# A two-layer transformer trunk: how the Down stage forms its weight sums, and when its first pieces are split

## The chip, the cores and the metric

The kernel runs on one core of a Trainium2 chip. A core has five engines with an instruction queue each: TensorE (PE, matrix products into PSUM banks), VectorE (DVE), ScalarE (ACT), GpSimd (POOL) and SyncE (SP), which issues most DMA transfers. Each queue runs in its written order. The metric is the device time of one execution in microseconds. The numbers come from that time and from the profile of one execution.

## The reference, cut to what matters

The trunk has two layers over 512 positions of width 1024. Each layer is an attention block and a SwiGLU block (FFN), each between an RMS norm before and after:

```
h = rms_norm(x, ffn_pre_g[layer])
f = (silu(h @ w_gate) * (h @ w_up)) @ w_down      # 1024 -> 2816 -> 1024
x = x + rms_norm(f, ffn_post_g[layer])
```

After layer 0, a shared key/value projection (w_kv_shared) is taken from x, for the attention of layer 1. All data are float32. For precision, each float32 operand is split into a high half and the rest, and a product is made of three matmuls: high by high, high by low, low by high.

## The kernel before, in words

**Split.** `split` (L143) makes the high half on ACT (a cast, L144) and the low half on DVE (a subtraction, L145). Weights give `whi` and `wlo`, hidden pieces `ph` and `pl`. `split_scaled` (L147) does the same with a factor per partition.

**Feed.** The class `Feed` brings the weights of the whole program in order. `load` issues the transfers some steps ahead. `split` (the method, L289) forms the sums a step needs, takes a pair of `hi`/`lo` tiles (three pairs are there) and splits. `next` asks for the split of the steps ahead of the one that PE takes now. Three weight streams matter here: `Pair` (gate and up weights of two hidden blocks), `Down` (w_down) and the plain chunks of w_v, whose gain was multiplied into the raw weights by DVE (L305) before the split.

**Pairs.** The hidden width is 22 blocks of 128. The first four are made whole, the other 18 in nine pairs (`products`, L1323) with a seven-product scheme that saves one product in eight. After each product j, ACT and DVE carry its banks into the tiles `gt` and `ut`; after j = 6 the two hidden blocks `hd` are finished (L1365 to L1369). `Hidden.add` (L1099) then forms their sums `hs` (L1113 to L1116).

**Down.** `down` (L1128) multiplies the hidden blocks by w_down with the same scheme. w_down is cut into four quarters: A11, A12, A21, A22. The seven products have the weights A11, A12, A22, E1, E2, E3, E6 in this order, with

```
E1 = A22 + A21,  E3 = A21 + A11,  E2 = E1 + A11,  E6 = E2 + A12
```

Each weight comes in six tiles (five of 1024 columns, a last one of 512), so Down has 42 steps: step 6 j + i is tile i of product j. A full step is 12 matmuls of 512 columns, a last one 6. Tiles 4 and 5 go together. The piece of step s + 2 is split when PE takes step s (`ahead`, L1135), and so is its weight.

**Where the sums came from.** A11 and A12 lie in tiles of 1024 (A12's last three in tiles of the pool "u"), and all were handed on as columns of 512. A22 is loaded to "u" tiles on SP (L218). E1 was made in place: once A22's tile was split, POOL issued a transfer that adds A21 from memory onto it (L231). For E3, SP loaded A21 to tiles with the tag "h", which hidden blocks leave, and POOL issued transfers that add A11 onto it. So a layer had 22 accumulating transfers. E2 and E6 are DVE sums (L236), tied to the steps 16 + 2 e and 27 + 2 e.

**After a product.** `After` (L1197) gathers the products into four row tiles of y: copies by ACT (L1211), sums by DVE (L1216), squares by ACT (L1221). After E3 rows 0 and 1 are whole, after E6 rows 2 and 3. `rstd` adds up the squares (L1249, L1250), takes the power -1/2 on POOL (L1252) and scales. In layer 0, `turn` (L1268) transposes the scaled y by PE (`yt`) and adds it to x; it stands in E6 behind group 2. In layer 1 (`AfterLast`), x is transposed by PE (`xt`, L1305) in E2, y gets its gain (L1311), and DVE scales, adds x (L1319) and stores the result (L1321).

**Buffers.** The pool "u" has 40 tiles of 128 x 512. Pieces, y tiles, x tiles, gate tiles and A22 share it.

**Order.** The program names engines and data. A planner with a cost model of its own puts the instructions of each engine and queue in an order, by program order among those it believes ready. So an instruction may stand earlier in a queue than the program has it, and the queue then holds whatever is behind it until its operands are there.

Of the kernel before, what the change touches and what calls it, by code (L numbers as in the profile page):

```python
# [68 lines left out]
def trunk(ctx: ExitStack, tc: tile.TileContext, a, out):  # L69
# [117 lines left out]
    class Down:  # L187
# [7 lines left out]

        def __init__(self, src):
            self.src, self.at = src, {}
# [5 lines left out]
        def quarter(self, j):  # L203
            return {self.A11: 0, self.A12: 1, self.A22: 3, self.E3: 2}.get(j)

        def load(self, j, i):
            q = self.quarter(j)
            if q is None:
                return
            n = self.width(i)  # L210
            src = self.src[q, i]
            tag = {self.A11: "raw" if i < 5 else "sum", self.A12: ("sum", "sum2", "sum2", "u", "u", "u")[i],
                   self.A22: "u", self.E3: "h"}[j]
# [6 lines left out]
            else:  # L220
# [8 lines left out]
        def accumulate(self, parts, q, i):  # L229
            for c, t in enumerate(parts):  # L230
                nc.gpsimd.dma_start(t, self.src[q, i, :, c * S:c * S + S], accum_op=OP.add)  # L231

        def plus(self, j, i, x, y):

            for t, u in zip(self.at[y, i], self.at[x, i]):
                V.tensor_tensor(t, t, u, op=OP.add)  # L236
            self.at[j, i] = self.at[y, i]

        def sums(self, j, i):

            s = self.TILES * j + i
            for e in range(self.TILES):
                if s == 16 + 2 * e:
                    self.plus(self.E2, e, self.E1, self.A11)
                if s == 27 + 2 * e:
                    self.plus(self.E6, e, self.E2, self.A12)

        def later(self, j, i):
            if j == self.A22:
                self.accumulate(self.at[j, i], 2, i)  # L250
                self.at[self.E1, i] = self.at[j, i]

    class Feed:
# [35 lines left out]
        def split(self, i):  # L289
            while len(self.ready) <= min(i, len(self.plan) - 1):  # L290
# [9 lines left out]
                elif isinstance(src, Pair):  # L300
                    src.sums(gain)
                    raw = src.raw[gain]
                elif gain is not None:
                    rv = raw[:, :n].rearrange("p (a b) -> p a b", a=gain.shape[1])
                    V.tensor_tensor(rv, rv, gain, op=OP.mult)  # L305
                if room is None:
# [4 lines left out]
                if isinstance(raw, list):  # L311
                    for c, t in enumerate(raw):
                        c_ = slice(c * S, c * S + S)
                        split(pieces[0][0][:, c_], pieces[0][1][:, c_], t)
                    src.later(*gain)
                for c in range(0, 0 if isinstance(raw, list) else n, w):
                    m = min(w, n - c)
                    with ExitStack() as st:
                        for b in self.behind.get(j, ()):
                            st.enter_context(tc.issue_after(b.ins))  # L320
                        split(pieces[c // w][0][:, :m], pieces[c // w][1][:, :m], raw[:, c:c + m])
# [392 lines left out]
    def plan_v(c):  # L714
        gv = gqk.rearrange("p (k t) -> p k t", t=2)
        for kc in range(4):
            feed.add(a["w_v"][c, kc], 1024, gv[:, 2 * kc:2 * kc + 2, 1:2].to_broadcast([P, 2, S]),
# [291 lines left out]
    def ffn(i, x_src, osp, firsts):  # L1009
# [73 lines left out]
        down(hid.pieces, post)  # L1083
# [3 lines left out]
    class Hidden:  # L1087
# [3 lines left out]
        def __init__(self, make):  # L1091
            self.make, self.n, self.t, self.two = make, 0, [], None
            self.pieces = {j: [] for j in range(7)}

# [33 lines left out]
    def down(pieces, post):  # L1128
# [3 lines left out]
        steps = [(j, i) for j in range(7) for i in range(Down.TILES)]  # L1132
        ready = {}

        def ahead(n):  # L1135
            while len(ready) <= min(n, len(steps) - 1):
                j, i = steps[len(ready)]
                h, l = U(F32R, "ph"), U(F32R, "pl")
                at = 0
                for t in pieces[j][i]:  # L1140
                    n_ = t.shape[1]
                    split(h[:, at:at + n_], l[:, at:at + n_], t)
                    at += n_
                ready[j, i] = h, l

        at = 0
        for j in range(7):
            to = (al, ga, de, be, al, al, be)[j]
            for group in ((0,), (1,), (2,), (3,), (4, 5)):
                got = []  # L1150
                for i in group:
                    ahead(at + 2 - len(got))
                    w = feed.next(Down.width(i), 2 - len(got))
                    got.append((i, w, ready[j, i]))
# [42 lines left out]
    class After:  # L1197
# [48 lines left out]
        def rstd(self, h):  # L1246
            q = slice(2 * h, 2 * h + 2)
            one, two = (1, 0) if h else (0, 1)
# [364 lines left out]
```

## Time and profile before

| what | us |
|---|---|
| median of 3 runs (1185.35 to 1186.72) | 1186.59 |
| profiled execution | 1186.21 |
| its span, first to last instruction | 1184.1 |
| PE, DVE, ACT, POOL busy | 1128.8, 947.1, 686.2, 62.5 |
| Down stage of layer 0, first matmul to the last of E6 | 425 to 554 |
| Down stage of layer 1 | 1040 to 1176 |

The span is what the trace shows; about 2 us of the time lie around it. "Idle before" a group is time in which its engine had nothing to run, with what ended it. PE's busy time holds matmuls that run at a low granted clock, so a full PE isn't always a fast one.

### The profile page before, as it was taken

The numbers are of one execution on the slowest core, as the hardware profiler recorded it, in microseconds if no ns is written. First come the engines' busy times: TensorE is split into PE (matmuls) and PEld (weight loads), VectorE is DVE, ScalarE is ACT, GpSimd is POOL, SyncE is SP. The second block draws the span as 40 slices with busy tenths as digits, with TensorE's granted clock in tenths as the row PEclk, the third lists the DMA queues.
The fourth block names the chain that finished last, engine by engine and source line by source line (L and its number), as shares of the span: only waits on it lengthen the run. The fifth ranks groups of instructions, "written<-read, shape, count | busy, mean of one in ns | idle before, by whom it ended". The sixth has DMA issues, their size and how long they took to land.

```text
span 1184.1 us, 18971 instructions
## 1 busy us (share of the span) xinstructions
PE 1128.8 (95%) x6973; PEld 998.9 (84%) x6973; DVE 947.1 (80%) x1712; ACT 686.2 (58%) x1361; POOL 62.5 (5%) x89
## 2 busy tenths in 40 slices
PE   9999999999999989798999999999999999988895
PEld 6788889899999977586888887789899999966774
DVE  7778648998989867799858877659989899776776
ACT  6476646655555556468437766556655555554563
POOL 1200000000000013100000000000000000013100
PEclk9999999999999999899999999999999999988898
DMA  7433154223232369532456656363232323378401
GB/s 227 117 107 89 37 182 153 75 90 125 90 125 90 120 189 229 139 99 89 147 142 168 166 142 170 89 214 125 72 125 90 107 94 105 133 226 182 116 1 72
DMA packets 62269, 149.79 MB, mean 127 GB/s; under 512 B 8352, under 2 KB 9888, under 8 KB 62176
## 3 DMA queue, kind: packets, MB, share of 16 engines
q1 hardware_dynamic: 55696, 137.00, 36.8%
q0 software_dynamic: 6336, 11.54, 5.7%
q8 instruction: 55, 0.90, 0.3%
q14 instruction: 38, 0.31, 0.1%
q10 hardware_dynamic: 144, 0.04, 0.0%
HBM read 125.28 MB, written 8.59 MB: 113 GB/s over the span
## 4 chain that ended last, share of the span: by engine, by line
PE 74%; issue 9%; DVE 6%; DMA 6%; ACT 3%; POOL 2%; SPq 0%; POOLq 0%; DVEq 0%; ACTq 0%
PE al L1349 18%; PE b L346 10%; PE b L347 10%; PE b L348 9%; PE be L1349 8%; DMA wd<-in_w_down 4%; PE ga L1349 4%; PE al L1162 4%; PE be L1162 2%; PE pt L498 2%; DVE wlo L145 1%; ACT whi L144 1%; POOL wd L231 1%; PE b L1474 1%; PE sc L1466 1%
## 5 line engine op out<-in xcount | busy, mean ns | idle before, releaser
L144 ACT CAST whi<-raw 128x1024 fp32r<-128x1024 f32 (+4 forms) x262 | 235.1, 907 | 247.3 <-PE al L1349 82.9
L145 DVE TENSOR_TENSOR wlo<-raw,whi 128x1024 fp32r<-128x1024 f32 (+4 forms) x262 | 271.0, 1042 | 81.9 <-ACT whi L144 80.1
L1349 PE MATMUL al<-th,whi 128*128 128x256 f32 x432 | 124.1, 287 | 0.0
L1349 PE MATMUL al<-tl,whi 128*128 128x256 f32 x432 | 122.2, 283 | 0.0
L1349 PE MATMUL al<-th,wlo 128*128 128x256 f32 x432 | 122.1, 283 | 0.0
L346 PE MATMUL b<-xh,whi 128*128 128x512 f32 (+1 forms) x304 | 116.4, 386 | 0.6 <-ACT xh L148 0.6
L347 PE MATMUL b<-xl,whi 128*128 128x512 f32 (+1 forms) x304 | 113.0, 372 | 0.0
L348 PE MATMUL b<-xh,wlo 128*128 128x512 f32 (+1 forms) x304 | 112.7, 371 | 0.0
L174 DVE TENSOR_TENSOR raw<-raw,raw 128x1024 f32<-128x1024 f32 x72 | 86.5, 1217 | 0.3 <-DMA raw<-in_w_pair 0.2
L1349 PEld LDWEIGHTS al<-th,whi 128*128 128x128 f32 x432 | 82.7, 191 | 1.8
L1349 PEld LDWEIGHTS al<-th,wlo 128*128 128x128 f32 x432 | 82.8, 192 | 0.0
L1349 PEld LDWEIGHTS al<-tl,whi 128*128 128x128 f32 x432 | 82.7, 192 | 0.0
L144 ACT CAST whi<-wd 128x512 fp32r<-128x512 f32 x86 | 50.6, 620 | 53.7 <-PE be L1162 14.9
L486 ACT ACTIVATE p<-p,mn 128x128 f32<-128x128 f32 (+1 forms) x96 | 54.0, 563 | 31.4 <-DVE mn L484 30.9
L145 DVE TENSOR_TENSOR ptl<-pt,pth 128x128 fp32r<-128x128 f32 (+1 forms) x96 | 46.2, 485 | 28.9 <-ACT pth L144 22.9
L145 DVE TENSOR_TENSOR wlo<-wd,whi 128x512 fp32r<-128x512 f32 x86 | 56.7, 685 | 14.6 <-ACT whi L144 14.6
L346 PEld LDWEIGHTS b<-xh,whi 128*128 128x128 f32 x304 | 57.6, 190 | 8.8 <-ACT xh L148 1.9
L231 POOL DMA_DIRECT2D wd<-in_w_down x44 | 39.0, 922 | 492.7 <-DMA wd<-in_w_down 222.7
L348 PEld LDWEIGHTS b<-xh,wlo 128*128 128x128 f32 x304 | 57.4, 189 | 8.9
L347 PEld LDWEIGHTS b<-xl,whi 128*128 128x128 f32 x304 | 57.7, 190 | 7.0 <-DVE xl L149 0.3
L1162 PE MATMUL al<-whi,ph 128*128 128x512 f32 x132 | 53.5, 405 | 8.6 <-ACT ph L144 7.0
L144 ACT CAST pth<-pt 128x128 fp32r<-128x128 f32 (+1 forms) x96 | 40.3, 424 | 28.7 <-PE pt L498 28.0
(301 smaller groups left out, 3297.8 us busy)
## 6 DMA issues: line engine op xcount, KB each, us to landing
raw<-in_w_pair SPq DMA_DIRECT2D x72, 512.0 KB, 3.6
wd<-in_w_down SPq DMA_DIRECT2D x54, 256.0 KB, 8.5
wd<-in_w_down POOLq DMA_DIRECT2D x44, 256.0 KB, 6.6
raw<-in_w_o SPq DMA_DIRECT2D x16, 512.0 KB, 3.6
raw<-in_w_gu SPq DMA_DIRECT2D x16, 512.0 KB, 3.9
raw<-in_w_down SPq DMA_DIRECT2D x16, 512.0 KB, 4.2
raw<-in_w_qkb SPq DMA_DIRECT2D x16, 512.0 KB, 3.5
x<-in_x SPq DMA_DIRECT2D x16, 256.0 KB, 5.9
```

Of the source, the lines that this page charges most:

```text
L144: return (nc.scalar.copy(dst_hi, src), V.tensor_tensor(dst_lo, src, dst_hi.bitcast(F32), op=OP.subtract))
L145: V.tensor_tensor(dst_lo, src, dst_hi.bitcast(F32), op=OP.subtract))
L174: V.tensor_tensor(t, x, y, op=OP.add)
L231: nc.gpsimd.dma_start(t, self.src[q, i, :, c * S:c * S + S], accum_op=OP.add)
L346: nc.tensor.matmul(o, l[0], r[0], start=start, stop=False)
L347: nc.tensor.matmul(o, l[0], r[1], start=False, stop=False)
L348: nc.tensor.matmul(o, l[1], r[0], start=False, stop=stop)
L486: nc.scalar.activation(p[:, :n], p[:, :n], AF.Exp, bias=mn[:, :1], scale=-1.0, accum_out=self.sums[:, qt:qt + 1])
L498: nc.tensor.transpose(t[:, kt * P:(kt + 1) * P], p[:, kt * P:(kt + 1) * P], ident)
L1162: nc.tensor.matmul(to[e], l[c], r[d], start=j < 4 and k == 0 and n == 0, stop=k == NF // 2 - 1 and n == 2, skip_group_check=True)
L1349: nc.tensor.matmul(o, l[c], r[d], start=first_ and n == 0, stop=k == K2 - 1 and n == 2, skip_group_check=True)
L1466: nc.tensor.matmul(o, q1[:, e, q_], k1[:, e, :n], start=True, stop=False)
```

## The change

- **E1 by DVE.** A21 is loaded once, by SP, to the "h" tiles, now as the load of E1's steps. DVE adds it onto A22's tiles, which gives E1. Then POOL issues the transfers that add A11 onto the A21 tiles, which gives E3. The accumulating transfers of a layer fall from 22 to 11.
- **A plan of the sums.** `PLAN` names the step at which each of the 18 tile sums (E1, E2, E6) is written.
- **Whole tiles.** Tiles of 1024 are handed on in one piece, so that a split or a sum of theirs is one instruction and not two.
- **First pieces.** `ahead` moves into `Hidden`. In the last pair, before the products 4, 5 and 6, it is called for the pieces of Down's steps 0 and 1.
- **w_v.** The gain goes into the split (`split_scaled`, in columns of 512), and the multiply L305 falls away for these eight chunks.
- **Norm.** `power` works on any run of row tiles. In layer 0, `turn` for rows 0 and 1 stands one group later. In layer 1, row 2 gets its power and scale as soon as its own sum is there, before row 3's.

```diff
+        PLAN = {**{s: (3, e) for e, s in enumerate((14, 15, 16, 18, 19, 21))},
+                **{s: (4, e) for e, s in enumerate((17, 20, 22, 24, 26, 28))},
+                **{s: (6, e) for e, s in enumerate((30, 32, 33, 35, 36, 38))}}
...
         def load(self, j, i):
-            q = self.quarter(j)
+            q = {self.A11: 0, self.A12: 1, self.A22: 3, self.E1: 2}.get(j)
...
-                   self.A22: "u", self.E3: "h"}[j]
+                   self.A22: "u", self.E1: "h"}[j]
...
-                parts = [t[:, c:c + S] for c in range(0, n, S)]
-            self.at[j, i] = parts
-            if j == self.E3:
-                self.accumulate(parts, 0, i)
+                parts = [t[:, :n]]
+            self.at["a21" if j == self.E1 else j, i] = parts
...
         def plus(self, j, i, x, y):
-            for t, u in zip(self.at[y, i], self.at[x, i]):
-                V.tensor_tensor(t, t, u, op=OP.add)
-            self.at[j, i] = self.at[y, i]
+            x, t = self.at[x, i], self.at[y, i]
+            n = max(len(x), len(t))
+            cut_ = lambda v: v if len(v) == n else [v[0][:, c * S:c * S + S] for c in range(n)]
+            for p, q in zip(cut_(t), cut_(x)):
+                V.tensor_tensor(p, p, q, op=OP.add)
+            self.at[j, i] = t
...
         def sums(self, j, i):
-            s = self.TILES * j + i
-            for e in range(self.TILES):
-                if s == 16 + 2 * e:
-                    self.plus(self.E2, e, self.E1, self.A11)
-                if s == 27 + 2 * e:
-                    self.plus(self.E6, e, self.E2, self.A12)
-
-        def later(self, j, i):
-            if j == self.A22:
-                self.accumulate(self.at[j, i], 2, i)
-                self.at[self.E1, i] = self.at[j, i]
+            j, e = self.PLAN.get(self.TILES * j + i, (None, 0))
+            if j == self.E1:
+                self.plus(j, e, "a21", self.A22)
+                t = self.at[self.E3, e] = self.at["a21", e]
+                for c, p in enumerate(t):
+                    nc.gpsimd.dma_start(p, self.src[0, e, :, c * S:c * S + S], accum_op=OP.add)
+            elif j == self.E2:
+                self.plus(j, e, self.E1, self.A11)
+            elif j == self.E6:
+                self.plus(j, e, self.E2, self.A12)
...
+                        for d in range(0, m, S):
+                            split_scaled(pieces[c // w][0][:, d:d + S], pieces[c // w][1][:, d:d + S],
+                                         raw[:, c + d:c + d + S], gain[:, (c + d) // S, 0:1])
...
     class Hidden:
+        def ahead(self, n):
+            while len(self.ready) <= min(n, len(self.STEPS) - 1):
+                j, i = self.STEPS[len(self.ready)]
+                h, l = U(F32R, "ph"), U(F32R, "pl")
...
     class After:
         def rstd(self, h):
...
+            self.power(2 * h, 2)
+
+        def power(self, i, n):
+            q = slice(i, i + n)
...
+            r = small("r")[:, :n]
+            nc.gpsimd.tensor_tensor(r, self.v[:, q], mhalf[:, :n], op=OP.pow)
+            for e in range(n):
+                self.scale(i + e, r[:, e:e + 1])
...
-            if j == Down.E6 and i == 2:
+            if j == Down.E6 and i == 3:
                 self.turn(0)
...
     class AfterLast(After):
         def whole(self, o, i):
...
+            if i >= 2 and not o:
+                self.power(i, 1)
...
     def products(xs, tb, rb, hid):
...
                 w = feed.next(1024, 2)
+                if p + 1 == pairs and j >= 4:
+                    hid.ahead(j // 5)
```

More of the change, by code (lines that the diff above doesn't have):

```diff
@@ L311, in split @@
                 if isinstance(raw, list):
[L312 to L313 removed]
+                    c = 0
+                    for t in raw:
+                        c_ = slice(c, c + t.shape[1])
                         split(pieces[0][0][:, c_], pieces[0][1][:, c_], t)
[L315 removed]
+                        c += t.shape[1]
                 for c in range(0, 0 if isinstance(raw, list) else n, w):
@@ L1093, in __init__ @@
             self.pieces = {j: [] for j in range(7)}
+            self.ready = []
+        STEPS = [(j, i) for j in range(7) for i in range(Down.TILES)]
+        def ahead(self, n):
+            while len(self.ready) <= min(n, len(self.STEPS) - 1):
+                j, i = self.STEPS[len(self.ready)]
+                h, l = U(F32R, "ph"), U(F32R, "pl")
+                c = 0
+                for t in self.pieces[j][i]:
+                    c_ = slice(c, c + t.shape[1])
+                    split(h[:, c_], l[:, c_], t)
+                    c += t.shape[1]
+                self.ready.append((h, l))
         def room(self):
@@ L1126, in add, with down @@
                     self.pieces[j].append([self.two[t]])
-    def down(pieces, post):
+    def down(hid, post):
         al, ga = [bank(name="al") for _ in range(2)], [bank(name="ga") for _ in range(2)]
         be, de = [bank("s", "be") for _ in range(2)], [bank("t", "de") for _ in range(2)]
[L1132 to L1144, printed above, removed]
         at = 0
```

54 lines of the change are left out of this document (23 added, 31 removed).

## The prediction

> **What bounds the kernel now.** I read the page first, for the shares of the engines and the chain of work that ended last. TensorE (PE) is busy for 95% of the span, and the chain holds almost nothing but matmuls, so a gain can only come from the places where PE waits. The changed stage runs twice, and these two stretches come out of the chain with "DMA wd<-in_w_down", which is a wait for weight sums.
>
> ```profile
> span 1184.1 us, 18971 instructions
> PE 1128.8 (95%) x6973; PEld 998.9 (84%) x6973; DVE 947.1 (80%) x1712; ACT 686.2 (58%) x1361; POOL 62.5 (5%) x89
> ```
>
> Then I read the order of PE's instructions through both Down stages (from 425 and from 1040 us): start, duration, and in brackets the idle time before and what ended it.
>
> ```profile
> 425.15 0.50 PE L1162 MATMUL al<-whi,ph 128*128 128x512 f32 x1 [3.48 <-ACT ph L144]
> 426.92 0.80 PE L1162 MATMUL al<-whi,pl 128*128 128x512 f32 x1 [1.04 <-DVE pl L145]
> 470.79 0.50 PE L1162 MATMUL de<-wlo,ph 128*128 128x512 f32 x1 [1.19 <-DVE wlo L145]
> 485.48 0.80 PE L1162 MATMUL be<-wlo,ph 128*128 128x512 f32 x1 [7.42 <-DVE wlo L145]
> 487.49 0.80 PE L1162 MATMUL be<-whi,pl 128*128 128x512 f32 x1 [1.22 <-DVE pl L145]
> 488.08 0.63 PE L1162 MATMUL be<-whi,ph 128*128 128x512 f32 x1
> 491.07 0.51 PE L1162 MATMUL be<-wlo,ph 128*128 128x512 f32 x1
> 535.85 0.44 PE L1277 MATMUL yt<-ident,y 128*128 128x128 f32 x2 [1.78 <-ACT y L1259]
> 538.07 0.30 PE L1277 MATMUL yt<-ident,y 128*128 128x128 f32 x1 [0.73 <-ACT ph L144]
> 1040.08 0.50 PE L1162 MATMUL al<-whi,ph 128*128 128x512 f32 x1 [3.48 <-ACT ph L144]
> 1041.85 0.80 PE L1162 MATMUL al<-whi,pl 128*128 128x512 f32 x1 [1.04 <-DVE pl L145]
> 1042.44 0.63 PE L1162 MATMUL al<-whi,ph 128*128 128x512 f32 x1
> 1047.56 0.46 PE L1162 MATMUL al<-whi,ph 128*128 128x512 f32 x1
> 1083.71 0.39 PE L1162 MATMUL de<-wlo,ph 128*128 128x512 f32 x1
> 1085.53 0.39 PE L1162 MATMUL de<-whi,ph 128*128 128x512 f32 x1
> 1090.26 0.80 PE L1162 MATMUL de<-wlo,ph 128*128 128x512 f32 x1 [4.34 <-DVE wlo L145]
> 1090.85 0.63 PE L1162 MATMUL de<-whi,pl 128*128 128x512 f32 x1
> 1095.12 0.56 PE L1162 MATMUL de<-whi,ph 128*128 128x512 f32 x1
> 1103.85 0.79 PE L1162 MATMUL be<-whi,pl 128*128 128x512 f32 x1 [3.70 <-DVE pl L145]
> 1104.44 0.63 PE L1162 MATMUL be<-whi,ph 128*128 128x512 f32 x1
> 1109.14 0.39 PE L1162 MATMUL be<-whi,pl 128*128 128x512 f32 x1
> ```
>
> Three kinds of stall stand here. At each entry of Down, PE waits for the first hidden piece (ph, pl). In products A22 and E1 it waits for DVE. In layer 0 product E6 it waits for the scaled y. Behind each long wait the clock is low: twelve matmuls start between 1042.44 and 1047.56, one every 0.427 us; without a wait before them, eight start between 1083.71 and 1085.53, one every 0.227.
>
> Why DVE is late is seen in the orders of DVE and POOL:
>
> ```profile
> 1081.49 2.68 POOL L231 DMA_DIRECT2D wd<-in_w_down  x3 [7.52 <-DVE wlo L145]
> 1102.79 0.86 POOL L231 DMA_DIRECT2D wd<-in_w_down  x1 [3.32 <-issue]
> 1087.62 0.69 DVE L236 TENSOR_TENSOR raw<-raw,wd 128x512 f32<-128x512 f32 x1 [5.90 <-DMA wd<-in_w_down]
> 1092.27 1.28 DVE L236 TENSOR_TENSOR raw<-raw,wd 128x512 f32<-128x512 f32 x2
> ```
>
> E1's eleven accumulating transfers start only at 1081.49 and are issued until 1102.79, about 2 us apart. The E2 sum (raw<-raw,wd) stands in DVE's queue and waits 5.90 us for one of them; the low halves (wlo) and pieces (pl) that PE needs are queued behind it.
>
> Last the windows by stage; the numbers are length, PE, PEld, DVE, ACT and POOL busy, granted clock, DMA share, GB/s.
>
> ```profile
> 425.10:458.00 32.90, 31.81 (x133) 25.95 (x134) 22.08 (x47) 19.47 (x47) 8.88 (x10) 0.95 0.94 275
> 458.00:491.00 33.00, 23.12 (x89) 17.30 (x88) 22.00 (x37) 15.87 (x31) 10.74 (x13) 0.85 0.90 181
> 491.00:535.00 44.00, 43.07 (x189) 35.20 (x187) 42.60 (x72) 28.81 (x58) 1.05 (x1) 1.00 0.25 78
> 535.00:555.00 20.00, 18.24 (x85) 14.41 (x86) 18.25 (x41) 15.69 (x34) 0.32 (x4) 1.00 0.16 55
> 555.00:580.00 25.00, 24.70 (x118) 19.80 (x117) 23.71 (x45) 13.67 (x35) 1.59 (x2) 1.00 0.54 188
> 1040.00:1074.00 34.00, 32.88 (x132) 26.62 (x133) 23.04 (x49) 19.17 (x46) 8.83 (x10) 0.90 0.94 266
> 1074.00:1104.00 30.00, 21.90 (x83) 16.67 (x81) 18.62 (x31) 16.07 (x31) 10.52 (x12) 0.86 0.84 168
> 1104.00:1157.00 53.00, 50.91 (x228) 41.68 (x228) 42.06 (x72) 32.25 (x65) 0.00 (x0) 0.95 0.10 27
> ```
>
> DMA is full (0.94) until about E1, and DVE is full from 491 to 535 (42.60 of 44) although PE loses nothing there. Where PE stalls (458 to 491, 1074 to 1104), neither DVE nor ACT is full: these are waits, not load.
>
> **First pieces inside the last pair.** Pieces 0 and 1 need hidden blocks that are long finished, so four casts and four 256-wide subtractions move from the entry into the last pair. There they cost DVE 4 x 0.35 us, by a row of seven:
>
> ```profile
> 1042.05 2.43 DVE L145 TENSOR_TENSOR pl<-hd,ph 128x256 fp32r<-128x256 f32 x7
> ```
>
>  PE then has two steps in hand, 24 matmuls x 0.227 = 5.4 us, in which the last hidden block and piece 2 are made. Removed per layer: 3.48 + 1.04 = 4.52 us of idle time, and the slow clock behind it: 12 x 0.20 = 2.4 us in layer 1; in layer 0, (1 - 0.95) x 32.90 = 1.6 us. That is 6.9 and 6.1. Next late is piece 2: DVE does the hidden sums first, and the moved work delays it by up to 1.4 us. I take off 0.5 per layer (bounds 0 and 1.4). Term: 13.0 - 1.0 = 12.0 us.
>
> **E1 summed by DVE.** Removed: 22 of the 44 accumulating transfers, and with them the wait of E2's sum behind POOL. Added per layer: 11 DVE adds of 512 columns. Two follow each other in 1.28 us, so one holds DVE for 0.60: 6.6 us per layer. The 11 plain loads of A21 are no new traffic: they replace E3's loads, on SP, into the same tag; but E3's 11 accumulates now wait for the adds. They are due 16 steps after the first add, some 41 us, and eleven need about 22. On POOL only its own later accumulates and the power operation of the norm queue behind them, and on SP the fetch of x stands behind A21's loads. The stalls that go: layer 0, 1.19 + 7.42 + 1.22 idle and 7 x 0.20 of slow clock (488.08 to 491.07), 11.2 us; layer 1, 4.34 + 3.70 idle, 10 x 0.20 of slow clock behind the first (1090.85 to 1095.12) and 11 x 0.20 behind the second (1104.44 to 1109.14), 12.2 us.
>
> The new wait is the add for A21's landing; the same step's wlo queues behind it, and PE behind that. The 27 loads of a stage are 7.1 MB; at the 266 GB/s of the first window of layer 1, that is 27 us. The first add is due some 30 us after the entry and needs only about the first 18 loads, so I price this wait at zero. Without that cover, it is the third rival.
>
> What comes in place is DVE's load. Layer 0, 458 to 555: 97.0 us long, DVE 22.00 + 42.60 + 18.25 = 82.9. After: + 6.6, less about 1 for 16 splits now made as one instruction of 1024 and not two of 512 (an estimate: two instructions overlap by 0.09, 0.69 against 0.60), less 3.7 for four w_v chunks (next part) = 84.8. PE needs 97.0 - 11.2 - 2.5 (next part) = 83.3. The densest stretch shows DVE 97% busy (491 to 535), so DVE needs 84.8 / 0.97 = 87.4 and gives back 4.1 us. Layer 1, 1074 to 1157: DVE 18.62 + 42.06 + 6.6 - 1 = 66.3, PE 83.0 - 12.2 = 70.8: enough on average. But steps 14 to 24 hold an add each bar one, with 1.8 + 1.2 = 3.0 us of DVE against 2.72 of PE, behind the 2.4 us of y and yg work at A12's end; less DVE's lead of two steps I get about 3 us late. The bounds are 0 and the density of 1104 to 1157 (0.79): 66.3 / 0.79 = 83.9, the whole 12.2 gone. I stay near the 0.97 row, since that is where DVE had a backlog. Term: 11.2 + 12.2 - 4.1 - 3.0 = 16.3 us.
>
> **Turn one group later, w_v, tail.** Layer 0's turn waited 1.78 + 0.73 us for the y scale; a step later, 2.72 us, y is there: 2.5 us. The w_v multiply goes into the split:
>
> ```profile
> L305 DVE TENSOR_TENSOR raw<-raw,gains 128x1024 f32<-128x1024 f32 x24 | 29.1, 1217 | 6.3 <-DMA raw<-in_w_qkb 6.2
> L149 DVE SCALAR_TENSOR_TENSOR xl<-x,gains,xh 128x512 fp32r<-128x512 f32 x8 | 6.0, 748 | 1.2 <-ACT xh L148 1.2
> 1178.21 2.74 DVE L1319 SCALAR_TENSOR_TENSOR yg<-yg,r,xt 128x512 f32<-128x512 f32 x4 [0.81 <-POOL r L1252]
> ```
>
> A chunk took two passes of 1.13 us (1217 ns less that overlap); now two fused ones of 0.67, the pitch of the last row: 0.9 less. On PE's path this is nothing by itself, as PE is 24.70 of 25.00 busy in 555 to 580; its use is in DVE's balance above. In the tail, the first row tile's power and scale run ahead of the second's. Best: two of the four scalings (1.3 us) leave the end. Worst: they stand in front of the second tile's y sum, 1.7 us late, a net loss of 0.4. I take 0.5.
>
> **Sum.** 12.0 + 16.3 + 2.5 + 0.5 = 31.3 us. The profiled execution took 1186.21 us, the median is 0.4 more: 1186.6 - 31.3 = 1155.3, rounded to 1155.
>
> A page's other price for the clock: the Trainium skill (TensorE: Matmul & The Clock Gate, Part 1) says that an idle window of about 3.4 us halves the clock until PE has been busy for about as long. The trace agrees in kind (waits over 3.4 us are followed by a pitch of 0.427, those of 1.19 and 1.78 us are not). By that rule each of the five stalls costs an estimated 1.7 us of clock, 8.5 against the 9.6 above, and the time would be 1156.
>
> **Rivals.** (1) DVE becomes the bound: at the density of 0.79 both layers give back their E1 gain and the turn (11.2 + 12.2 + 2.5, of which 7.1 is already off), +18.8: 1174; halfway 1165. For it: DVE is full from 491 on. Against it: it has gaps now where the adds go. 20%.
>
> (2) The entry does not shorten, since piece 2, a weight half or a PSUM bank is next late: 12.0 less gain, 1167. Against it: the weight halves of steps 0 to 2 are made before the pair ends. 8%.
>
> (3) Slower: the adds stand in DVE's queue before A21 has landed. An add blocks DVE as E2's did, 5.90 us at worst; 12 tile sums x 5.90 = 71 us against some 39 removed: 1155 + 71 - 7 (what DVE's load no longer adds) = 1219. It decides from a mean wait of 3.2 us per sum. For it: DMA share 0.94 until E1. Against it: the accumulates that slowed these loads are gone. 6%; a mild form, 1 us each, gives 1155 + 12 = 1167 and has 8%.
>
> (4) It doesn't do what it says, since the planner keeps E3's transfers ahead of A21's on SP: nothing gained in E1, 1155 + 16 = 1171. 3%.
>
> (5) The Trainium skill (SBUF — State Buffer, Who interferes with whom) says that a DVE instruction with two SBUF inputs blocks with a GpSimd one that reads SBUF. As a mechanism of this kernel: each of the 22 adds stands still for one of POOL's issues, 0.86 us in the row of 1102.79, 19 us, 1174. The trace speaks against it: the E2 sums ran at 0.69 us among those issues. 2%.
>
> **How the numbers follow.** The forecast (1144 to 1164) has 53%; its low end is all stalls gone and no load of DVE's. The range 1144 to 1175 takes in (1), (2), (5), (4) and the mild (3). A difference under 0.2%, 2.4 us, cannot be told from none here. Slower is the hard form of (3), 0.06, and 0.02 for what I have not seen; no change takes 0.04, where (1) and a part of (3) come together; faster has 0.88.
>
> **What would show it.** Right: no PE idle over 1 us at either entry; no DVE idle ended by "DMA wd" in E1; 22 accumulates, all behind the adds; waits in A22 to E2 under 3 us. Wrong: DVE idle before the new adds, PE idle at step 2, or x late for its transposes in E2 of layer 1.

## The result, and the profile after

The changed kernel takes 1154.11 us (median of 4 runs, 1153.01 to 1155.78), the kernel before 1185.97 (4 runs, 1184.71 to 1186.72): a ratio of 0.9734, 95% interval 0.9717 to 0.9750. The forecast was 1155, the range 1144 to 1175. The profiled execution took 1154.28 us.

The first lines of the page after:

```profile
span 1152.5 us, 18913 instructions
PE 1119.8 (97%) x6973; PEld 993.6 (86%) x6973; DVE 948.1 (82%) x1696; ACT 683.4 (59%) x1335; POOL 44.1 (4%) x68
```

PE executes the same 6973 matmuls. The span fell by 31.6 us, and DVE's work is what it was (947.1 before): only waits, and the slow clock behind them, went. PE's order through both Down stages after (start, duration, and in brackets the idle time before):

```profile
421.18 0.28 PE L1363 MATMUL be<-xh,wlo 128*128 128x256 f32 x1
421.30 0.40 PE L1166 MATMUL al<-whi,ph 128*128 128x512 f32 x1
...
483.85 0.50 PE L1166 MATMUL al<-whi,ph 128*128 128x512 f32 x1 [2.25 <-ACT ph L144]
...
518.45 0.39 PE L1166 MATMUL be<-whi,pl 128*128 128x512 f32 x1
521.17 0.44 PE L1285 MATMUL yt<-ident,y 128*128 128x128 f32 x2 [2.33 <-ACT y L1267]
522.39 1.40 PE L1285 MATMUL yt<-ident,y 128*128 128x128 f32 x6 [0.79 <-ACT y L1267]
...
1023.29 0.28 PE L1363 MATMUL be<-xh,wlo 128*128 128x256 f32 x1
1023.41 0.40 PE L1166 MATMUL al<-whi,ph 128*128 128x512 f32 x1
...
1087.04 0.50 PE L1166 MATMUL al<-whi,ph 128*128 128x512 f32 x1 [1.42 <-ACT ph L144]
...
1107.60 0.50 PE L1166 MATMUL al<-whi,ph 128*128 128x512 f32 x1 [1.64 <-ACT y L1215]
...
1126.54 0.50 PE L1166 MATMUL be<-whi,ph 128*128 128x512 f32 x1 [0.98 <-ACT ph L144]
...
1131.24 0.73 PE L1166 MATMUL be<-whi,pl 128*128 128x512 f32 x2 [1.78 <-DVE pl L145]
```

Both entries of Down are without a wait (421.18 to 421.30, 1023.29 to 1023.41). The waits for E1's weight sums are gone too. What is left stands at the entry of E2, at the turn of layer 0, and in layer 1 between E2 and E3 and in E6.

Read in stages, each running from one product's first matmul to the next one's, this is where the 31.6 us went. "Entry" runs from the last matmul of the last pair to A12; "rest of layer 0" from E6's first matmul to the first pair of layer 1, since the planner lets E6 and the products of w_v overlap.

| us, layer 0 / layer 1 | before | after | gain |
|---|---|---|---|
| entry and A11 | 21.5 / 22.9 | 15.1 / 15.2 | 6.4 / 7.7 |
| A22 | 17.1 / 22.5 | 15.1 / 15.2 | 1.9 / 7.3 |
| E1 | 26.2 / 21.6 | 17.5 / 18.4 | 8.8 / 3.2 |
| E2 | 15.0 / 20.4 | 17.1 / 20.6 | -2.1 / -0.2 |
| rest of layer 0 | 322.5 | 324.7 | -2.2 |
| E6 of layer 1 | 21.6 | 21.0 | 0.6 |

A12, E3, the pairs and the tail each stand within 0.25 us of where they were. A product without waits takes 14.96 us.

### The profile page after: what moved, and what is told of

Same layout as the page of the kernel before. It is cut to its first block, busy times and chain, and to the rows that moved or that the text cites. A ratio compares the mean times of both kernels' runs of the same rounds, so it can differ in the third digit from the quotient of the medians.

```text
span 1152.5 us, 18913 instructions
## 1 busy us (share of the span) xinstructions
PE 1119.8 (97%) x6973; PEld 993.6 (86%) x6973; DVE 948.1 (82%) x1696; ACT 683.4 (59%) x1335; POOL 44.1 (4%) x68
## 4 chain that ended last, share of the span: by engine, by line
PE 78%; DVE 10%; issue 6%; ACT 4%; POOL 1%; DMA 1%; DVEq 0%; POOLq 0%; SPq 0%; ACTq 0%
PE al L1363 18%; PE b L349 10%; PE b L350 10%; PE b L351 10%; PE be L1363 9%; PE al L1166 5%; PE ga L1363 4%; DVE wlo L145 3%; PE ga L1166 2%; PE pt L501 2%; PE be L1166 1%; ACT whi L144 1%; DVE pl L145 1%; DVE wd L233 1%; PE b L1488 1%
## 5 line engine op out<-in xcount | busy, mean ns | idle before, releaser
L144 ACT CAST whi<-raw 128x1024 fp32r<-128x1024 f32 (+4 forms) x224 | 224.8, 1005 | 234.3 <-PE al L1363 81.0
L145 DVE TENSOR_TENSOR wlo<-raw,whi 128x1024 fp32r<-128x1024 f32 (+4 forms) x224 | 260.7, 1165 | 74.0 <-ACT whi L144 71.9
L489 ACT ACTIVATE p<-p,mn 128x128 f32<-128x128 f32 (+1 forms) x96 | 54.0, 563 | 31.6 <-DVE mn L487 31.2
L144 ACT CAST whi<-wd 128x512 fp32r<-128x512 f32 x86 | 50.5, 620 | 34.4 <-PE be L1166 10.6
L1166 PE MATMUL al<-whi,pl 128*128 128x512 f32 x132 | 52.1, 398 | 0.7 <-DVE pl L145 0.7
```

Of the source, the lines that this page charges most:

```text
L144: return (nc.scalar.copy(dst_hi, src), V.tensor_tensor(dst_lo, src, dst_hi.bitcast(F32), op=OP.subtract))
L145: V.tensor_tensor(dst_lo, src, dst_hi.bitcast(F32), op=OP.subtract))
L489: nc.scalar.activation(p[:, :n], p[:, :n], AF.Exp, bias=mn[:, :1], scale=-1.0, accum_out=self.sums[:, qt:qt + 1])
L1166: nc.tensor.matmul(to[e], l[c], r[d], start=j < 4 and k == 0 and n == 0, stop=k == NF // 2 - 1 and n == 2, skip_group_check=True)
```

## The experiments

All times below are medians of 4 runs (6 in one case), each kernel in alternation with the kernel before on its chip (1186 to 1187.5 us there). The lengths of products and of stages are taken as in the table above.

| kernel | us | ratio to before, 95% interval |
|---|---|---|
| changed kernel | 1154.11 | 0.9734 (0.9717 to 0.9750) |
| a1_no_early_pieces | 1168.22 | 0.9843 (0.9820 to 0.9866) |
| b1_early_pieces_only | 1165.42 | 0.9828 (0.9802 to 0.9854) |
| b2_sums_only | 1174.37 | 0.9896 (0.9872 to 0.9921) |
| b3_e3_behind_e1 | 1167.84 | 0.9842 (0.9816 to 0.9867) |
| b4_early_and_queue | 1155.19 | 0.9742 (0.9722 to 0.9763) |
| a9_e2_sums_late | 1147.12 | 0.9668 (0.9645 to 0.9692) |
| a6_e6_sums_on_pool | 1177.94 | 0.9925 (0.9894 to 0.9957) |
| a10_turn_behind_group2 | 1161.20 | 0.9788 (0.9765 to 0.9811) |
| a5_wv_multiply_apart | 1157.71 | 0.9755 (0.9740 to 0.9770) |
| a11_pieces_before_y | 1140.10 | 0.9603 (0.9587 to 0.9619) |
| a15_pieces_and_turn | 1141.09 | 0.9615 (0.9601 to 0.9630) |
| a16_all | 1139.49 | 0.9598 (0.9584 to 0.9612) |

### One part alone, or one part away

**a1_no_early_pieces**, the changed kernel without

```diff
-                if p + 1 == pairs and j >= 4:
-                    hid.ahead(j // 5)
```

> The changed kernel without the early pieces: Down's first two pieces are split behind the last pair again. If the entry stall is a term of its own, each entry of Down idles again for 3.5 + 1.0 us with a slow clock behind it, 6.4 us in layer 0 and 7.7 in layer 1 (the start of E's first product and its length, before against after), and the time is 1154 + 14 = 1168. Rival: DVE's load bounds what follows, so that time lost at the entry lets DVE get ahead and comes back in E1 and E2, at most some 5 us: 1163.

It takes 1168.22, as the prediction's steps had it. The entries and A11 take 22.2 and 22.9 us in place of 15.1 and 15.2; the other stages stay within 0.5 us of the changed kernel's. The early pieces are worth some 14 us of the 32.

**b1_early_pieces_only**, the kernel before with that call and the class `Hidden` that it needs:

> The kernel before with the early pieces alone. If the entry is a term of its own: 1186 - 14 = 1172. Rival: PE then comes to A22 and E1 6 to 8 us sooner in each layer while the accumulating transfers keep their own pace, so that the stall only moves there: entry 0.1 us, but E1 longer than 26.2 (layer 0) and A22 longer than 22.5 (layer 1) by up to the same amount, time 1180 to 1186.

It is better than both: 1165.42. Beside the entries (15.1 and 15.4), E1 of layer 0 fell from 26.2 to 22.3 and E1 of layer 1 from 21.6 to 15.0 us, with no sum moved; A22 of layer 1 stays long (21.9). SP's order of layer 1, first one row of the kernel before, then this kernel's, and then POOL's in this kernel, have

```profile
1041.82 1.95 SPq L218 DMA_DIRECT2D wd<-in_w_down  x4
...
1016.44 0.33 SPq L218 DMA_DIRECT2D wd<-in_w_down  x1
...
1032.41 7.86 SPq L218 DMA_DIRECT2D wd<-in_w_down  x14
```

```profile
1022.08 0.95 POOL L231 DMA_DIRECT2D wd<-in_w_down  x1 [196.21 <-DVE ut L1364]
...
1080.14 0.86 POOL L231 DMA_DIRECT2D wd<-in_w_down  x1 [2.51 <-DVE wlo L145]
```

The loads of the stage's tiles (L218) now begin 10.6 us ahead of A11's first matmul (1027.02), inside the last pair, and POOL's transfers 4.9 us ahead of it. Before, the loads began 1.7 us behind A11's first matmul (1041.82 and 1040.08), and POOL's transfers 5.5 us behind it (1045.62). The last one is issued at 1080.14, where E1 begins (1079.14). So the early pieces also start the stage's transfers earlier. The other runs agree: in every kernel with early pieces the first of these loads is issued 10.5 to 10.6 us ahead of A11, in every kernel without them (before, a1, b2, b3) 1.7 to 2.7 us behind it. The prediction had no term for that.

**b2_sums_only**, the kernel before with the changed class `Down` (A21 loaded as E1's load, E1 by DVE, `PLAN`, whole tiles):

> The kernel before with the new sums alone (E1 by DVE, the plan of the sums, whole tiles), without the early pieces, the fused w_v, the later turn and the new tail. If the parts add: A22 and E1 come down to about 15.2 and 17 to 18 us in both layers, 1186 - 18 = 1168. If the early pieces are needed to bring the transfers forward: A21 lands later, DVE idles before its adds, and the gain is under 12 us, 1174 or more.

A22 and E1 came down as in the changed kernel (15.1 and 17.2; 15.2 and 18.4). But it takes 1174.37, the second theory's number, though not for its reason: DVE waits for no transfer in A22 and E1. The entry and A11 grew from 21.5 to 23.0 in layer 0, and the rest of layer 0 from 322.5 to 330.2. That rest is not for want of the early pieces, since a1_no_early_pieces has 324.6 there; about half of it is a wait of 4.17 us at the second half of the turn (0.29 before), which a5_wv_multiply_apart has too (below). The parts do not add up one by one.

### What made E1 late

**b3_e3_behind_e1**, the kernel before with one binding on POOL's queue:

```diff
             for c, t in enumerate(parts):
-                nc.gpsimd.dma_start(t, ..., accum_op=OP.add)
+                with ExitStack() as st:
+                    if q == 0:
+                        st.enter_context(tc.issue_after(self.last.ins))
+                    d = nc.gpsimd.dma_start(t, ..., accum_op=OP.add)
+                if q == 2:
+                    self.last = d
```

> The kernel before, with POOL's transfers for E3 issued behind those for E1; nothing else. It tells whether E1 was late for POOL's queue order or for the accumulating transfers as such. If for the order: E1's first transfer is issued some 7 us sooner in layer 1, DVE's wait of 5.9 us goes, and 7 us or more are gained, 1179 or less. If eleven transfers at 2 us each behind A22's splits are late by themselves: E1 still waits, and the gain is 0 to 4 us, 1182 to 1186.

It takes 1167.84, well inside the first theory's 1179 or less. Here are POOL's transfers in layer 1, first of the kernel before, then of this one:

```profile
1045.62 1.86 POOL L231 DMA_DIRECT2D wd<-in_w_down  x2 [209.49 <-DMA wd<-in_w_down]
1056.63 0.86 POOL L231 DMA_DIRECT2D wd<-in_w_down  x1 [9.15 <-DMA wd<-in_w_down]
...
1073.10 0.88 POOL L231 DMA_DIRECT2D wd<-in_w_down  x1 [1.13 <-DVE y L1216]
1081.49 2.68 POOL L231 DMA_DIRECT2D wd<-in_w_down  x3 [7.52 <-DVE wlo L145]
```

```profile
1067.25 1.86 POOL L234 DMA_DIRECT2D wd<-in_w_down  x2 [235.80 <-DVE wlo L145]
```

Before, the ten transfers from 1045.62 to 1073.10 and the first of the three at 1081.49 are E3's. They wait for their loads of A21, and E1's eleven, which PE needs two products sooner, stand behind the last of them. The 7.52 us are put down to a low half of DVE, but the chain of the kernel before has the last of these loads there, which lands at 1080.82:

```profile
1069.60 11.22 DMA wd<-in_w_down
...
1081.52 2.65 POOL wd L231 x3
```

In the second order E1's first two go out at 1067.25, 14.9 us sooner than E1's first before (1082.12); 4.1 of that is the whole stage's earlier place (A11 at 1036.00, not 1040.08). A22 of layer 1 falls from 22.5 to 17.1 (layer 0 had 17.1 already), E1 to 17.1 and 15.0. So the 7.52 us of POOL were neither the transfers' own cost nor a lack of DVE sums, but a queue in the wrong order.

**b4_early_and_queue** puts that binding and the early pieces together, still with all 22 accumulating transfers and no E1 sum by DVE:

> The kernel before with two edits and no sum of E1 by DVE: the first pieces are made inside the last pair, and on POOL the accumulating transfers of E3 are issued behind those of E1. Theory (the stalls of A22 and E1 came from POOL's queue order, so DVE's sums are not what removed them): the entries give 14.1 us and the order gives what it gave alone in A22 and E1 (9.1 in layer 0; 5.4 + 6.6 in layer 1), 1187 - 35 = 1152, at or under the changed kernel's 1154; A22 and E1 at most 17.2 us long in both layers. Rival (the sums of E1 must come from DVE, since PE now reaches E1 3.6 us sooner and the accumulating transfers are late for it): waits of 4 us and more come back in A22 or E1, and the time is 1160 or more.

1155.19, against 1154.11 for the changed kernel; the intervals of the two ratios overlap. The theory holds in its main point, though not in its last 3 us: E1 has one wait of 1.74 us in layer 0 and is without any in layer 1 (14.96 us). A22 and E1 together take 66.7 us over both layers here and 66.2 in the changed kernel (87.3 before). That the sums are made by DVE is thus not what the change gains by. It is one way of two to get E3's loads out of the way of E1.

### What the sums by DVE cost

**a9_e2_sums_late**:

```diff
-                **{s: (4, e) for e, s in enumerate((17, 20, 22, 24, 26, 28))},
+                **{s: (4, e) for e, s in enumerate((23, 24, 25, 26, 27, 28))},
```

> The changed kernel with the sums of E2 dealt out six steps later (steps 23 to 28, and not 17 to 28 between those of E1). In layer 0 PE waits 2.63 and 0.73 us at the entry of E2, behind sums of E1 and E2 that DVE makes from 475 to 482. If that is an order (sums not yet needed stand ahead of the low halves and pieces that are): this wait goes and 2 to 4 us come off, 1151. If it is load (DVE has no free time from 466 to 485 in whatever order): the wait moves a few steps on, 1154 or more.

1147.12, 7 us under the changed kernel: it is an order. DVE's queue in the changed kernel ahead of the wait at 483.85 (`raw<-raw,wd` is a sum of E2):

```profile
475.45 1.28 DVE L233 TENSOR_TENSOR raw<-raw,wd 128x512 f32<-128x512 f32 x2
...
478.79 1.28 DVE L233 TENSOR_TENSOR raw<-raw,wd 128x512 f32<-128x512 f32 x2
480.00 1.22 DVE L145 TENSOR_TENSOR wlo<-raw,whi 128x1024 fp32r<-128x1024 f32 x1
```

and ACT's:

```profile
481.29 1.99 ACT L144 CAST whi<-raw 128x1024 fp32r<-128x1024 f32 x2 [2.68 <-DVE wlo L145]
483.18 0.61 ACT L144 CAST ph<-hs 128x512 fp32r<-128x512 f32 x1
```

Four additions, 2.4 us at 0.60 each, stand in front of the low half at 480.00. ACT waits 2.68 us for that one, and the piece (ph) that PE needs at 483.85 is queued behind ACT's wait. The windows of E1 and of E2 with E3 in layer 0 (length, PE, PEld, DVE, ACT, POOL busy, granted clock, DMA share, GB/s), first after, then a9_e2_sums_late:

```profile
466.40:483.80 17.40, 15.20 (x67) 12.11 (x65) 17.40 (x29) 10.94 (x20) 3.28 (x4) 1.00 0.78 190
483.80:516.00 32.20, 31.82 (x133) 25.89 (x134) 28.63 (x43) 18.84 (x35) 0.00 (x0) 0.95 0.34 107
```

```profile
466.80:481.80 15.00, 15.00 (x67) 12.40 (x67) 15.00 (x26) 9.43 (x18) 2.92 (x4) 1.00 0.94 227
481.80:512.00 30.20, 30.20 (x133) 24.56 (x132) 29.85 (x45) 20.23 (x37) 0.00 (x0) 1.00 0.27 91
```

With the sums later, DVE is busy for 44.85 of 45.20 us and PE loses nothing. A full DVE costs PE time only where something not yet due stands ahead of something due. E1 of layer 1 fell from 18.4 to 16.1.

**a6_e6_sums_on_pool**, E6's sums by POOL:

```diff
-                self.plus(j, e, self.E2, self.A12)
+                self.plus(j, e, self.E2, self.A12, nc.gpsimd)
```

> The changed kernel with the six sums of E6 formed by POOL and not by DVE, which takes about 11 additions of 0.60 us from DVE in each layer. If DVE's load is what the layers still give back from E2 to the turn (waits of 1.06 to 2.72 us at the turn of layer 0 and 1.4 to 2.2 us in E6 of layer 1): 1149 to 1151. If these waits are an order of the queues and not a load: 1153 to 1156. If an addition of DVE and one of POOL with two SBUF inputs block one another, as the fifth rival has it: DVE's instructions of 0.68 us grow where POOL adds, and the time is over 1157.

1177.94, 24 us slower by the medians. The profiled execution lost 20.3 us, and E2 alone lost as much (29.3 and 29.1 us long, 17.1 and 20.6 in the changed kernel). DVE's order and POOL's in layer 0, and then one POOL row of layer 1:

```profile
492.21 12.42 DVE L145 TENSOR_TENSOR wlo<-raw,whi 128x1024 fp32r<-128x1024 f32 x1 [2.46 <-ACT whi L144]
```

```profile
491.47 2.73 POOL L233 TENSOR_TENSOR raw<-raw,raw 128x1024 f32<-128x1024 f32 x1
...
494.43 3.05 POOL L233 TENSOR_TENSOR raw<-raw,raw 128x1024 f32<-128x1024 f32 x1
496.79 6.75 POOL L233 TENSOR_TENSOR wd<-wd,raw 128x512 f32<-128x512 f32 x5
...
1079.81 25.14 POOL L233 TENSOR_TENSOR raw<-raw,raw 128x1024 f32<-128x1024 f32 x1 [0.49 <-ACT whi L144]
```

A subtraction that takes DVE 1.22 us elsewhere took 12.42 and ended 1 us behind POOL's last addition (503.54). In layer 1 an addition that takes POOL 2.73 us elsewhere took 25.14, while DVE ran its subtractions and additions without a gap (1079.59 to 1102.68), each at its usual length. Each of the two engines stands still here while the other goes on, over several instructions.

### The turn

The prediction took the program's "one group later" for PE's order. It is not. PE's order holds twelve matmuls of E6 in front of the first transposes in both kernels (515.96 to 518.45 after, 531.19 to 533.68 before), since the planner moves the transposes up.

**a10_turn_behind_group2**, the changed kernel with the transposes of a turn bound behind the last matmul of E6's third group:

```diff
+                        with tc.issue_after(self.last.ins):
+                            nc.tensor.transpose(...)
```

> The changed kernel with layer 0's turn bound behind the third group of E6's matmuls on PE's own queue. In the kernels before and after, the first eight transposes stand behind the same twelve matmuls of E6, whatever group the program names. Theory (the turn still waits because the planner left its first half where it was; the scaled y is there at 522.3, and 36 matmuls end at about 524): the waits of 2.72 and 1.06 us and the slow clock behind them go, 4 to 6 us: 1149. Rival (DVE or ACT is the bound in this stretch, and what PE gains at the turn is lost at the first products of w_v): 1153 to 1155.

Both fell: 1161.20, 7 us slower than the changed kernel. PE's order in it, and ACT's:

```profile
523.99 0.80 PE L1166 MATMUL be<-whi,ph 128*128 128x512 f32 x1 [4.46 <-ACT ph L144]
550.99 0.69 PE L1286 MATMUL yt<-ident,y 128*128 128x128 f32 x2 [2.92 <-ACT y L1267]
```

```profile
518.22 0.62 ACT L1225 ACTIVATE sq<-y 128x512 f32<-128x512 f32 x1
...
521.08 2.56 ACT L1267 ACTIVATE y<-y,r 128x512 f32<-128x512 f32 x4 [0.92 <-POOL r L1260]
523.55 1.92 ACT L144 CAST ph<-hd 128x256 fp32r<-128x256 f32 x6
```

The transposes were not the only thing that came late. The pieces of E6's next steps (ph) stand on ACT behind the squares and the four scalings. With the transposes out of the way, PE waits for the pieces instead, and longer. The wait at 550.99 is another, in the second half of the turn; a5_wv_multiply_apart has it too.

**a11_pieces_before_y**, on top of a9_e2_sums_late:

```diff
                 post.during(j, group[0])
+            if j == Down.E3:
+                hid.ahead(at + 2)
             post.product(j, to)
```

> The kernel with E2's sums six steps later (a9_e2_sums_late, 1147.1) and with the pieces of E6's steps 36 to 38 asked for before the y sums of E3's end. In it PE still waits for pieces in E6: 2.15 us in layer 0; 1.37, 2.19 and 1.01 in layer 1. Theory (the pieces stand on ACT and DVE behind squares, y products and scalings that PE does not need yet): these waits go, 4 us in layer 1 and up to 2 in layer 0, 1141 to 1143. Rival (ACT and DVE are full here, and the y chain is late instead: the wait for the scaled y at the turn grows by as much): 1146 to 1148.

1140.10, a little better than expected. E6 of layer 1 takes 16.6 in place of 22.3 us, the rest of layer 0 321.1 in place of 323.2. The planner also moved the first transposes behind 48 matmuls by itself, and PE executes them without a wait:

```profile
523.61 1.03 PE L1287 MATMUL yt<-ident,y 128*128 128x128 f32 x8
```

**a15_pieces_and_turn** adds the binding of the turn (36 matmuls):

> The kernel of a11_pieces_before_y, and its first eight transposes of the turn bound behind 36 matmuls of E6. Theory (in a10_turn_behind_group2 the binding lost only since the pieces were late on ACT; with the pieces first, PE has 8.2 us of E6 to do while y is scaled): the wait at the turn of layer 0 goes, 2 to 4 us under a11_pieces_before_y, about 1140. Rival (what it loses in a10_turn_behind_group2 is the later half of the turn, with x late for the products of w_v): slower than a11_pieces_before_y by 3 us or more.

1141.09: neither theory. There was no wait at the first transposes left to remove.

**a16_all** adds the banks of E2 and the tail:

```diff
-            to = (al, ga, de, be, al, al, be)[j]
+            to = (al, ga, de, be, ga, al, be)[j]
...
-            if i >= 2 and not o:
-                self.power(i, 1)
...
+            self.power(2, 1)
+            with first(100):
+                self.power(3, 1)
```

> The kernel of a15_pieces_and_turn with two more edits. E2 goes into the PSUM banks of A12, not those of A11 that E3 needs right behind it: the wait of 1.9 us between E2 and E3 of layer 1, for the copy of y, goes. In the tail the y sums of both row tiles stand ahead of the scalings of the first: the 8.87 us from the last matmul of Down to the end becomes 7.7 to 8.3. Together 2.0 to 3.0 us under a15_pieces_and_turn, 1137 to 1139 if that one meets its theory. If these places are hidden anyway: the same time as a15_pieces_and_turn.

1139.49, 1.6 us under a15_pieces_and_turn, where 2.0 to 3.0 were expected; the intervals of the two ratios overlap. In this kernel E2 is added onto A12's product in the bank and not onto A11's, so y holds other numbers; its time is read for the two waits alone. The wait of 1.9 us between E2 and E3 of layer 1 is gone (E2 takes 18.5 in place of 20.4), and the stretch from the last matmul of Down to the end went from 8.87 to 8.52 us, less than expected. DVE in its tail, and in the changed kernel's:

```profile
1130.02 0.75 DVE L1337 SCALAR_TENSOR_TENSOR yg<-yg,r,xt 128x512 f32<-128x512 f32 x1 [0.66 <-POOL r L1262]
1130.69 0.68 DVE L1222 TENSOR_TENSOR y<-y,be 128x512 f32<-128x512 f32 x1
```

```profile
1144.32 1.42 DVE L1332 SCALAR_TENSOR_TENSOR yg<-yg,r,xt 128x512 f32<-128x512 f32 x2 [0.66 <-POOL r L1260]
1145.65 0.68 DVE L1220 TENSOR_TENSOR y<-y,be 128x512 f32<-128x512 f32 x1
```

Only one of the two scalings was moved behind the y sum.

### The multiply of w_v

**a5_wv_multiply_apart**:

```diff
-                elif gain is not None and gain.shape[1] > 2:
+                elif gain is not None:
...
-            feed.add(a["w_v"][c, kc], 1024, gv[:, 2 * kc:2 * kc + 2, 1:2],
+            feed.add(a["w_v"][c, kc], 1024, gv[:, 2 * kc:2 * kc + 2, 1:2].to_broadcast([P, 2, S]),
```

> The changed kernel with the gain of w_v multiplied by DVE in a pass of its own again, and then split, as before. Priced at nothing on PE's path and at 0.9 us of DVE for each chunk, 3.7 us in all. If nothing hangs on it: 1154 to 1155. If DVE is the bound from E3 to the products of w_v in layer 0: 1157 to 1159, with longer waits for wlo and x in that stretch.

1157.71, 3.6 us slower by the medians, 2.5 by the ratios; the intervals of the two ratios overlap from 0.9740 to 0.9750, so the time alone does not settle it. It falls into the second theory's range. The rest of layer 0 takes 328.8 us in place of 324.7, with this wait at the second half of the turn, among the products of w_v (PE's order, then ACT's and POOL's):

```profile
545.80 0.69 PE L1285 MATMUL yt<-ident,y 128*128 128x128 f32 x2 [3.60 <-ACT y L1267]
```

```profile
544.42 2.56 ACT L1267 ACTIVATE y<-y,r 128x512 f32<-128x512 f32 x4 [4.49 <-POOL r L1260]
```

```profile
540.17 4.22 POOL L1260 TENSOR_TENSOR r<-ssv,mhalf 128x2 f32<-128x2 f32 x1 [18.91 <-DVE ssv L1258]
```

The trace goes further than either theory. The scalings wait for the power operation on POOL. It takes 1.07 us at this place in the changed kernel, where PE waits 0.32, and 4.22 us here, while DVE runs two subtractions of w_v, a low half of weights, an addition and the multiply, all with two inputs in SBUF. It ends 0.56 us after that multiply, about as long as a power operation takes with DVE idle (0.55 us for one column in the tail after, 0.70 for two in the tail before). The same operation took 4.82 us in b2_sums_only and 3.35 in a10_turn_behind_group2, and these three kernels have the longest rest of layer 0 (328.8 us here, then 330.2 and 332.0, the last with the wait at 523.99 in it); in all the others it took 0.95 or 1.07, and the rest is 321 to 325. No run moved the power operation to another engine, so this is read from the traces and not tried apart.

## Why the prediction was right, and where it was not

The time was right to 1 us, and the two large terms were real. Their reasons were half right, and the small terms were not.

- **Entry: right.** 14.1 us measured, 12.0 predicted. Neither the last hidden block nor piece 2 was late, so the 0.5 a layer taken off was not paid, and A11 is a full 15 us. a1_no_early_pieces confirms it. The term left out is in b1_early_pieces_only: the stage's transfers start earlier as well, and E1 fell by 3.9 and 6.6 us where it still came by POOL.
- **The stalls of A22 and E1: right in what they are worth, wrong in what made them.** 23.4 us were listed. The products took 27.5 us over 14.96 each before, and 6.4 after, nearly all of it from another cause (the point after next). "E1's eleven accumulating transfers start only at 1081.49" was the right row (the first of its three is E3's last), but the prediction read it as the cost of having them, and named E2's sum behind POOL as the wait that counts. b3_e3_behind_e1 and b4_early_and_queue show that POOL's queue was in the wrong order: with E1's transfers first, the same 22 do as well as DVE's sums.
- **The wait of the adds for A21: right at zero.** DVE waited for no DMA from 446 to 486 or from 1048 to 1088. The third rival fell.
- **DVE's load: near in size, wrong in kind.** The prediction gave back 7.1 us by DVE's density. What came back in E1 and E2, against 14.96 and against before, is 2.5 and 2.1 us in layer 0 and 3.4 and 0.2 in layer 1, 8.2 in all. But a9_e2_sums_late gains 7 us with the same instructions and a DVE that is busier than 0.97. The step that failed is "DVE needs 84.8 / 0.97": a density seen where PE lost nothing was made a price. That 7.1 came near 8.2 is luck. The clue stood in the prediction's own windows: "DVE is full from 491 to 535 (42.60 of 44) although PE loses nothing there". The first rival falls with it.
- **The turn: wrong.** 2.5 us gained was predicted; the rest of layer 0 got 2.2 longer. The step "a step later, 2.72 us, y is there" took a place in the program for a place in PE's queue, although the section on the order says how the planner moves things. The chain from E3's end to the first scaled y also grew: from E6's first matmul to the first scaling it was 3.9 us (531.19 to 535.08) and is 4.4 (515.96 to 520.39). The 0.5 us are in the power operation on POOL, which took 1.62 us in place of 1.10. DVE began to make its operand 2.5 us after E6's first matmul both times. Both times the operation ended 0.57 to 0.58 us behind the DVE subtraction that ran when it began, and that is one of a whole 1024 tile now (518.56, 1.22 us) and was one of 512 before (533.78, 0.68). And rows are scaled one after the other, so the second transposes wait 0.79 for the third scaling. Here are ACT and POOL, before and then after:

```profile
535.08 2.56 ACT L1259 ACTIVATE y<-y,r 128x512 f32<-128x512 f32 x4 [0.18 <-POOL r L1252]
...
533.95 1.10 POOL r L1252
```

```profile
520.39 2.56 ACT L1267 ACTIVATE y<-y,r 128x512 f32<-128x512 f32 x4 [0.92 <-POOL r L1260]
...
518.73 1.62 POOL L1260 TENSOR_TENSOR r<-ssv,mhalf 128x2 f32<-128x2 f32 x1 [42.44 <-DVE ssv L1258]
```

- **w_v: too small.** "On PE's path this is nothing by itself" is not what a5 shows: beside the new sums, a multiply apart costs some 3 us, as POOL's power operation, and with it the second half of the turn, is late among the products of w_v. In the kernel before, where it stood apart too, PE waited only 0.29 us there. The term was sought in DVE's balance and lay in what stands beside POOL's operation.
- **Tail: nothing.** 0.5 us predicted, none measured (8.82 before, 8.87 after). The worst order of the two came: both scalings of row 2 stand ahead of row 3's y sum (1144.32 and 1145.65).
- **The fifth rival: not here, but near.** In the changed kernel the 44 additions among POOL's transfers take 0.68 us each, so issuing does not hold them up. a6 shows the same two engines excluding each other once POOL computes, and so do the power operations of a5, b2 and a10, which the prediction counted only as standing in a queue. This agrees with the Trainium skill (SBUF — State Buffer, Who interferes with whom), which says that a DVE instruction with two SBUF inputs and a GpSimd one that reads SBUF share an exclusive lock.

Of the signs named ahead, all for "right" were there: no wait at either entry, no wait of DVE for A21, 22 accumulating transfers behind their additions, and no wait over 2.25 us in A22 to E2. Of those for "wrong", x late for its transposes in layer 1's E2 did not come (20.6 us, 20.4 before).

The errors of the sum: +2.1 (entry), +2.5 (A22, E1 and E2: 21.1 - 2.3 = 18.8 against 16.3), -4.7 (turn), -0.5 (tail), and +0.9 in E6 of layer 1 and smaller places. They come to the 0.3 us between 31.6 and 31.3. Such an agreement is luck, not proof.

What stays open: that the early pieces bring the stage's loads forward is seen in every run, but why by that much was not tried. That POOL's power operation is what makes the second half of the turn late in a5, b2 and a10 is read from their traces alone. In a15_pieces_and_turn E6 of layer 0 took 4.3 us longer than in a11_pieces_before_y, and all but 1.4 was made up before layer 1's first pair; why was not tried.

## What to carry to other kernels

When an engine that issues transfers idles, write down what stands in its queue in order, and what each waits for, before moving the work to another engine: one binding of the order gave as much here as a new way to form the sums. Price a busy engine by what stands ahead of the thing that is due, not by its density; the best kernel here, a11_pieces_before_y at 1140.10 us (0.9603 of before, interval 0.9587 to 0.9619), does the work of the changed kernel in another order and is 14 us faster. Where a planner orders the queues, a place in the program is only a wish: read the place in the engine's own order before pricing a move. And where POOL has even a small operation on the path, look at what DVE runs beside it.

## What the runs showed of the hardware that was not expected

- Additions by POOL and subtractions by DVE, both with two inputs in SBUF, do not share time but shut each other out for many instructions in a row: 12.42 us for a 1.22 us subtraction of DVE while POOL made seven additions, and 25.14 us for a 2.73 us addition of POOL (a6_e6_sums_on_pool). A power operation of two columns on POOL, 0.70 us with DVE idle, took 4.22 us beside DVE's string of five such instructions in a5_wv_multiply_apart, and 4.82 in b2_sums_only.
- Issuing transfers on POOL does not do this: the 44 additions of E1 and E2 in the changed kernel took 0.68 to 0.69 us each, those beside an issue of POOL's 11 accumulating transfers a layer as well.
- The slow clock came behind waits shorter than the 3.48 us and more of the prediction's list. In the changed kernel, behind the idle 2.25 us at 483.85 and 0.33 at 485.38, matmuls start 0.43 us apart from 485.97 to 488.11, and the window up to 516 has a granted clock of 0.95. Behind 1.42 us at 1087.04 they start 0.23 apart.
